# Layer 0's last modulation chunks as sums on VectorE, part of the exponentials' sums on GpSimd, and norms by quarters of the tokens

## Chip, cores and metric

The kernel runs on one core of a Trainium2 chip. The metric is the device time of one execution in microseconds. The engines are called PE (TensorE's matmuls), PEld (its weight loads), DVE (VectorE), ACT (ScalarE), POOL (GpSimd) and SP (SyncE, which issues the transfers here).

## The reference

Two layers work on 512 latent tokens and a prefix of 256 context tokens, 1024 wide, in fp32. Layer 0 is attention (16 query heads, 4 key heads, head size 64), layer 1 a bidirectional Mamba-2 mixer; each is followed by a gated FFN with a short convolution.

```python
for i in range(DEPTH):
    mod_l = split((silu(c) @ ada_w[i] + ada_b[i]), 6)          # shift, scale, gate: mixer, then FFN
    mod_c = split(silu(c_ctx) @ ada_w[i] + ada_b[i], 6)
    h_l = modulate(rms_norm(x, norm_mix_w[i]), mod_l[0], mod_l[1])
    h_c = modulate(rms_norm(ctx, norm_mix_w[i]), mod_c[0], mod_c[1])
    ...                                                        # attention or Mamba-2
    x = x + mod_l[2] * o_l
    x = x + mod_l[5] * conv_ffn(modulate(rms_norm(x, norm_ffn_w[i]), mod_l[3], mod_l[4]))
    ...                                                        # the context likewise, in layer 0
```

In attention, queries and keys are normed per head (`rms_norm` over 64 channels), rotated by their position (latent tokens only), and a softmax runs over 512 latent and 256 context keys for latent queries, over the 256 context keys for context queries.

## The kernel before

Activations lie transposed: 128 channels on the partitions, tokens along the row (512 latent and 256 context columns, T = 768). Products that need fp32 accuracy split each operand in a high and a low part (`split`: ACT rounds to the high part, VectorE or GpSimd subtracts) and make three passes (`mm3`). The instructions of each engine are put in order by a scheduler that follows the program's order as a priority and lets an idle engine take later work; in the first stage the order of PE, ACT and VectorE is that of the program, and `keep_in_program_order` pins single instructions elsewhere.

**Modulation.** Layer 0's chunks 0 and 1 (shift and scale of the mixer) are made by `ada` on PE during the first projections. Chunks 2, 3 and 4 are six further `ada` units in the list `fill`: each loads four tiles of 512 KB from `adaB`, multiplies them with the conditioning vectors `sc32` (eight matmuls of 512 columns into four groups of 32 rows, L128), copies the result (L130), transposes and adds it up with four small matmuls (L134), and adds the bias (`modulation`). Layer 0's chunk 5 and all of layer 1 are made by `ada_dve` during layer 0's FFN: a row of the transposed weight matrix times the conditioning vector, summed along the row on VectorE (L167).

**Norms.** `rstd_rows` makes 1/sqrt(mean of squares). It multiplies each tile of 128 tokens, as the stationary operand, with one or two columns of ones (L236), so that tokens lie on partitions and the following operations are 1 to 12 columns wide (L239 to L244); then it spreads the result (L247) and transposes it back, tile by tile (L253). It is used for the tokens' norms (width 1024 or 2048) and for the heads' norms in `normed`.

**Attention.** Eight pairs of heads (`Pair`). `maxima` makes the scores once in a rough form to find each query's maximum on VectorE (L603). `steps` runs seven steps: scores with the maximum taken off (L673, L675), the exponential on ACT into `pr` (L676, three buffers), and the sum of the exponentials over the key tiles in `acc`, on VectorE: step 1 adds the first two (L681), steps 2 to 5 add to it (L683), step 6 sums the context's (L687). The product with the values (L637) comes a step later; after step 5 PE adds `acc` over the partitions (L643) and the output is divided. Scores and maxima share two PSUM buffers.

Between the steps, `fill.run(us)` takes work from a list: the projections of queries 4 to 7 (L105 to L108 into `ps_q`), the norms of queries and keys (`normed`: squares on ACT, an exchange of rows by four transfers into `qsw` at L532, the rotary products on GpSimd at L533 to L535, the norm, and the product L539), the modulation units, and from pair 6 on the output projection. Its order is `"123a4k5a6a7aaa"`, with `us = 1.75` up to pair 5. Big weight tiles come from one set of ten buffers (`t4`); transfers are issued on SP's queue in order.

Of the kernel before, what the change touches and what calls it, by code (L numbers as in the profile page):

```python
# [7 lines left out]
P = 128  # L8
# [49 lines left out]
CST_IDENT, CST_BLK, CST_SEL, CST_COS, CST_SIN = 0, 128, 130, 132, 132 + L  # L58
NCST = 132 + 2 * L
# [51 lines left out]
def ada(g, src, layer, chunks, m0, nm, big=True):  # L111


    nc = g.nc
    cols = nm * len(chunks) * P
    per = (1024 if big else T) // cols
    st = []
    for k0 in range(0, KT, per):
        n = min(per, KT - k0)
        t = t4(g, "wada") if big else t3(g, "wada")  # L120
        t = t[:, : n * cols].rearrange("p (k a b) -> p k a b", k=n, a=len(chunks))
        nc.sync.dma_start(t.rearrange("p k a b -> p (k a b)"), src[:, k0 * cols : (k0 + n) * cols])
        st += [t[:, k].rearrange("p a b -> p (a b)") for k in range(n)]
    yield 0
    ps = Bank(g, "ps_ada")
    for k in range(KT):
        j = k % 4
        nc.tensor.matmul(ps[32 * j : 32 * j + 32, 0:cols], g.sc32[:, k, :], st[k], start=k < 4, stop=k >= 4)  # L128
    sb = g.t3p.tile([P, 512], F32, tag="t2", bufs=6, name="ada_sb")
    nc.vector.tensor_copy(sb[:, 0:cols], ps[:, 0:cols])  # L130
    yield BREAK
    pt = Bank(g, "ps_adt")
    for i in range(cols // P):
        nc.tensor.matmul(pt[:, 2 * i : 2 * i + 2], sb[:, i * P : (i + 1) * P], g.sel, start=True, stop=True)  # L134
    for i, ch in enumerate(chunks):
        modulation(g, pt[:, 2 * nm * i : 2 * nm * (i + 1)].rearrange("p (m v) -> p m v", v=2), layer, ch, m0, nm)
    yield BREAK
# [15 lines left out]
def ada_dve(g):  # L153


    nc = g.nc
    cb = g.t3p.tile([P, 2 * D], F32, name="cb")
    nc.sync.dma_start(cb, g.I["cflat"].broadcast_to([P, 2 * D]))
    follow(g, nc.scalar.activation(cb, cb, AF.Silu))
    for layer, ch, nv in [(0, 5, 2)] + [(1, ch, 2 if ch < 2 else 1) for ch in range(6)]:  # L160
        md = g.mod[layer][ch]
        for m in range(KT):
            w = g.t3p.tile([P, D], F32, tag="wada", bufs=3, name="wada")
            nc.sync.dma_start(w, g.I["adaT"][(ch + 1 if layer else 0) * KT + m])
            for v in range(nv):
                junk = g.t3p.tile([P, D], F32, tag="junk", bufs=1, name="junk")
                g.tc.keep_in_program_order(nc.vector.scalar_tensor_tensor(  # L167
                    junk, w, 1.0, cb[:, v * D : (v + 1) * D], ALU.mult, ALU.mult, accum_out=md[:, m, v : v + 1]))
                yield
        modulation(g, md[:, :, :nv], layer, ch, 0, KT, nv)  # L170
# [56 lines left out]
def rstd_rows(g, sq, n, cols, width, name, bank):  # L227

    nc = g.nc
    c = cols.shape[-1]
    nt = n // P
    ps = bank(f"ss{name}")
    for t in range(nt):
        nc.tensor.matmul(ps[:, t * c : (t + 1) * c], sq[:, t * P : (t + 1) * P], cols, start=True, stop=True)  # L236
    small = lambda nm: g.p.tile([P, nt * c], F32, tag="rst", bufs=8, name=nm)
    a, y, u = small("rsa"), small("rsy"), small("rsu")
    nc.vector.tensor_scalar(a, ps[:, : nt * c], 1.0 / width, EPS, ALU.mult, ALU.add)  # L239
# [5 lines left out]
    rb = t3(g, f"rb{name}", n=n)  # L245
    wide = lambda v: v.unsqueeze(2).broadcast_to([P, nt * c, P // c])
    nc.vector.scalar_tensor_tensor(rb.rearrange("p (a b) -> p a b", b=P // c), wide(u), 1.5, wide(y), ALU.add, ALU.mult)  # L247
    yield BREAK
    out = []
    for t0 in range(0, nt, 4):  # L250
        pt = bank(f"rsT{name}")
        for t in range(t0, min(nt, t0 + 4)):
            nc.tensor.transpose(pt[:, (t - t0) * P : (t - t0 + 1) * P], rb[:, t * P : (t + 1) * P], g.ident)  # L253
        yield (pt, t0 * P, min(n, (t0 + 4) * P))
# [55 lines left out]
class Norm:  # L310
# [23 lines left out]
    def gen(self, seg, x, lag=2):  # L334

        i, a, b = seg
        g, nc, n = self.g, self.g.nc, b - a
        for _ in range(lag):
            yield
        rows = rstd_rows(g, self.acc[seg, 6], n, g.ones[:, :1], D, self.name, lambda nm: Bank(g, nm))  # L340
        next(rows)
        for _ in range(lag):
            yield
        rs = t3(g, f"rs{self.name}", n=n)
        nc.scalar.copy(rs, next(rows)[0][:, :n])
# [33 lines left out]
def attention(g, fill, X, late):  # L379
# [14 lines left out]
    mods = [ada(g, I["adaA"][m], 0, (0, 1), m, 1, big=False) for m in range(KT)]  # L394
# [26 lines left out]
    nc.sync.dma_start(g.cst, I["cst"][:, :CST_COS])  # L421
# [9 lines left out]
    def warmth(n):  # L431
        for _ in range(n):
            nc.tensor.matmul(warm[:, :P], g.ones, g.ones, start=True, stop=True)
# [8 lines left out]
    norm = rstd_rows(g, acc, L, g.ones[:, :1], D, "a", Bk)  # L442
# [12 lines left out]
    rsl, _, _ = next(norm)  # L455
# [12 lines left out]
    for m in range(KT):  # L468
# [11 lines left out]
        if m == 3:  # L480
            norm = rstd_rows(g, sqc, C, g.ones[:, :1], D, "a", Bk)
            next(norm)
        if m == 4:
            rsc = t3(g, "rsc", n=C)
            pt, _, _ = next(norm)
            nc.scalar.copy(rsc, pt[:, :C])
# [15 lines left out]
    man.__exit__(None, None, None)  # L502
    nc.sync.dma_start(g.cs, I["cst"][:, CST_COS:])

# [20 lines left out]
    def normed(qs, gain, eng):  # L525
# [10 lines left out]
        for r in rstd_rows(g, sq, T, g.blk, HD, "q", Bk):  # L536
            if r is not BREAK:
                pt, c0, c1 = r
                nc.vector.tensor_tensor(qs[:, c0:c1], qs[:, c0:c1], pt[:, : c1 - c0], ALU.mult)  # L539
            yield BREAK  # L540
# [18 lines left out]
    def queries(p, qs, eng):  # L559
# [14 lines left out]
        split(g, qs, *qprep[p])  # L574
        yield 0

    onesr = g.const.tile([P, P], F32R, name="onesr")
    nc.scalar.copy(onesr, g.ones)
# [5 lines left out]
    class Pair:  # L584
# [43 lines left out]
        def steps(self):  # L628
# [10 lines left out]
            def final(po, ps, acc, out):  # L639

                n = out.shape[-1]
                for e in range(2):
                    nc.tensor.matmul(ps[S64[e], :n], g.ones[:, :HD], acc[:, n * e : n * e + n], start=True, stop=True)  # L643
# [22 lines left out]
            for t in range(7):  # L666
                ps, pr = Sb("ps_s"), g.t3p.tile([P, 1024], F32, tag="pr", bufs=3, name="pr")
                for q0, n, k0, off in (((0, L, t * P, 0),) if t < 6 else ((L, C, L, 0), (L, C, L + P, C))):
# [5 lines left out]
                    for e in range(2):  # L674
                        nc.tensor.matmul(outs[e], onesr[S64[e]], self.diag[S64[e], q], start=False, stop=True)  # L675
# [3 lines left out]
                elif t == 1:  # L679
                    acc = g.t3p.tile([P, 1024], F32, tag="acc", bufs=1, name="acc")  # L680
                    nc.vector.tensor_tensor(acc, prev, pr, ALU.add)  # L681
                elif t < 6:
                    nc.vector.tensor_tensor(acc, acc, pr, ALU.add)  # L683
# [10 lines left out]
    for n, j in enumerate((0, 1, 2, 4, 5, 3)):  # L694
# [8 lines left out]
        for gen in early:  # L703
            next(gen, None)
    vals = values()
# [20 lines left out]
    adas = list(fill.q)  # L726
    fill.q = [kgen if o == "k" else adas.pop(0) if o == "a" else qgen[int(o)] for o in "123a4k5a6a7aaa"]
# [151 lines left out]
def ssd(g, x, norm, wf, bg, close):  # L879
# [340 lines left out]
    norm = rstd_rows(g, acc[0], L, g.ones[:, :1], 2 * D, "y", lambda nm: Bank(g, nm))  # L1220
    next(norm)
    m_tile(4, ws, ps, 0, L, range(2 * 4, 16))
    nc.scalar.copy(rs, next(norm)[0])
# [31 lines left out]
def body(nc, tc, I, out, dbg=None):  # L1255
# [20 lines left out]
    g.ident, g.blk, g.sel = (cst[:, a:b] for a, b in  # L1276
                             ((CST_IDENT, CST_IDENT + P), (CST_BLK, CST_BLK + 2), (CST_SEL, CST_SEL + 2)))
    g.ones = g.const.tile([P, P], F32, name="ones")
    nc.vector.memset(g.ones, 1.0)
# [8 lines left out]
    for i in range(6):  # L1288
# [157 lines left out]
```

## Time and profile before

| | us |
|---|---|
| median of 3 runs | 1912.97 |
| lowest, highest | 1905.94, 1915.4 |
| the profiled execution | 1914.7 |
| its span | 1912.9 |

The span is from the first to the last instruction of the profiled execution. Tables of windows give each engine's busy time in a stretch, in us from the start of the span; attention lies in about 5 to 400 us, its head pairs in about 122 to 400 us. Groups are given as line, engine, operation, tile names, shapes and count, then busy time and mean duration in ns, then the idle time before them. Rows of a single line or tile give min/median/max in ns instead. A busy PE counts matmuls as the profile models them.

### The profile page before, as it was taken

The page shows a single profiled execution, that of the slowest core. Times are in us where ns is not written, and L with a number is a line of the kernel's source. Part 1 is how long each engine was busy: PE and PEld are TensorE (multiplying, and loading weights), DVE is VectorE, ACT ScalarE, POOL GpSimd, SP SyncE. Part 2 cuts the span into 40 slices and gives each one's busy share as a digit, 9 for nine tenths or more (in the row PEclk, how much of TensorE's full clock was granted, in tenths as well). Part 3 has the DMA queues.
Part 4 walks back from the last instruction along what each step waited for, and adds up shares of the span by engine and source line. Part 5 has one row for each costly group of instructions (what it writes and reads, how often), then busy time and mean ns, then how long its engine had stood idle before and what let it go on. Part 6 is the DMA issues. An engine that isn't in the chain of part 4 may idle for free.

```text
span 1912.9 us, 27512 instructions
## 1 busy us (share of the span) xinstructions
PE 1876.5 (98%) x10834; PEld 1547.6 (81%) x10834; DVE 1311.2 (69%) x1943; ACT 823.0 (43%) x1426; POOL 309.8 (16%) x274
## 2 busy tenths in 40 slices
PE   9999999999999999999999999999999999999999
PEld 7866555678888888888888888888888878888887
DVE  5578778678877777444488777777888466565555
ACT  3634444255122222222266777776667352323331
POOL 2241111031000000000040344443434210000000
PEclk9989998999999999999999999999999999999999
DMA  9221332114434555221122443334443322323232
GB/s 337 78 89 45 113 112 95 34 45 166 132 122 132 174 188 166 66 67 60 62 89 87 121 118 115 126 113 133 120 138 115 91 77 86 102 88 110 88 100 88
DMA packets 73425, 210.02 MB, mean 110 GB/s; under 512 B 8912, under 2 KB 14416, under 8 KB 73168
## 3 DMA queue, kind: packets, MB, share of 16 engines
q1 hardware_dynamic: 73296, 208.26, 34.3%
q8 instruction: 85, 1.39, 0.3%
q14 instruction: 44, 0.36, 0.1%
HBM read 198.79 MB, written 6.82 MB: 107 GB/s over the span
## 4 chain that ended last, share of the span: by engine, by line
PE 79%; DVE 9%; issue 3%; ACT 2%; POOL 1%; DMA 1%; DVEq 0%; SPq 0%; POOLq 0%; ACTq 0%
PE ps_up L106 10%; PE ps_up L108 10%; PE ps_up L105 10%; PE ps_d L105 6%; PE ps_d L106 6%; PE ps_d L108 6%; PE ps_in L106 4%; PE ps_in L108 4%; PE ps_in L105 4%; PE ps_o L637 2%; PE ps_s L673 2%; PE ps_st L1033 2%; DVE ht L281 1%; PE ps_wo L108 1%; PE ps_wo L105 1%
## 5 line engine op out<-in xcount | busy, mean ns | idle before, releaser
L87 DVE TENSOR_TENSOR wl<-wst,wh 128x1024 fp32r<-128x1024 f32 x205 | 254.5, 1242 | 244.9 <-PE ps_up L106 137.7
L85 ACT CAST wh<-wst 128x1024 fp32r<-128x1024 f32 x211 | 221.2, 1049 | 423.2 <-DMA wst<-in_wup 333.8
L106 PE MATMUL ps_up<-hlf,wh 128*128 128x512 f32 x1008 | 357.0, 354 | 0.0
L105 PE MATMUL ps_up<-hhf,wh 128*128 128x512 f32 x1008 | 356.9, 354 | 0.0
L108 PE MATMUL ps_up<-hhf,wl 128*128 128x512 f32 x1008 | 356.8, 354 | 0.0
L105 PEld LDWEIGHTS ps_up<-hhf,wh 128*128 128x128 f32 x1008 | 190.5, 189 | 26.5
L106 PEld LDWEIGHTS ps_up<-hlf,wh 128*128 128x128 f32 x1008 | 190.6, 189 | 26.4
L108 PEld LDWEIGHTS ps_up<-hhf,wl 128*128 128x128 f32 x1008 | 190.5, 189 | 26.4
L105 PE MATMUL ps_in<-hhs,wh 128*128 128x512 f32 (+1 forms) x560 | 204.4, 365 | 0.0
L106 PE MATMUL ps_in<-hls,wh 128*128 128x512 f32 (+1 forms) x560 | 199.4, 356 | 0.0
L108 PE MATMUL ps_in<-hhs,wl 128*128 128x512 f32 (+1 forms) x560 | 198.7, 355 | 0.0
L105 PE MATMUL ps_d<-hdh,wh 128*128 128x512 f32 (+1 forms) x568 | 193.6, 343 | 1.4 <-DVE X L784 1.2
L108 PE MATMUL ps_d<-hdh,wl 128*128 128x512 f32 (+1 forms) x568 | 193.5, 341 | 0.0
L106 PE MATMUL ps_d<-hdl,wh 128*128 128x512 f32 (+1 forms) x568 | 193.0, 340 | 0.3 <-DVE hdl L87 0.3
L784 DVE SCALAR_TENSOR_TENSOR X<-ps_d,mod,X 128x512 f32<-128x512 f32 (+1 forms) x224 | 124.6, 583 | 36.9 <-PE ps_d L108 36.6
L106 PEld LDWEIGHTS ps_d<-hdl,wh 128*128 128x128 f32 x568 | 106.6, 188 | 14.8 <-DVE hdl L87 0.7
L105 PEld LDWEIGHTS ps_d<-hdh,wh 128*128 128x128 f32 x568 | 106.3, 188 | 14.8 <-DVE X L784 1.4
L105 PEld LDWEIGHTS ps_in<-hhs,wh 128*128 128x128 f32 x560 | 105.9, 189 | 15.1 <-issue 1.2
L108 PEld LDWEIGHTS ps_in<-hhs,wl 128*128 128x128 f32 x560 | 105.8, 189 | 14.8
L108 PEld LDWEIGHTS ps_d<-hdh,wl 128*128 128x128 f32 x568 | 106.7, 188 | 13.1
L106 PEld LDWEIGHTS ps_in<-hls,wh 128*128 128x128 f32 x560 | 106.0, 189 | 13.2
L676 ACT ACTIVATE pr<-ps_s 128x1024 f32<-128x1024 f32 x56 | 57.2, 1021 | 110.6 <-PE ps_s L675 109.6
(340 smaller groups left out, 3547.3 us busy)
## 6 DMA issues: line engine op xcount, KB each, us to landing
wst<-in_wup SPq DMA_DIRECT2D x88, 512.0 KB, 3.6
wada<-in_adaT SPq DMA_DIRECT2D x56, 512.0 KB, 3.9
wst<-in_win SPq DMA_DIRECT2D x48, 512.0 KB, 3.7
wst<-in_wdown SPq DMA_DIRECT2D x44, 512.0 KB, 3.6
E<-ad SPq DMA_DIRECT2D x64, 256.0 KB, 6.8
wada<-in_adaB SPq DMA_DIRECT2D x24, 512.0 KB, 4.6
ec<-ead SPq DMA_DIRECT2D x64, 128.0 KB, 5.0
wst<-in_wout SPq DMA_DIRECT2D x16, 512.0 KB, 3.6
```

What stands on the lines that cost most here:

```text
L85: keep(nc.scalar.copy(hi, src))
L87: keep(eng.tensor_tensor(lo, src, _r(hi), ALU.subtract))
L105: mm(out, wh, ah, start=first, stop=False)
L106: mm(out, wh, al, start=False, stop=False)
L108: mm(out, wl, ah, start=False, stop=last)
L281: nc.vector.scalar_tensor_tensor(t[:, c0:c1], ap, g.moda[layer][ca][:, m, v : v + 1], rs[:, c0:c1], ALU.mult, ALU.mult)
L637: nc.tensor.matmul(po[S64[e], :n], v, pr[:, 512 * e + off : 512 * e + off + n], start=first, stop=last)
L673: nc.tensor.matmul(outs[e], a[S64[e], k], b[S64[e], q], start=i == 0, stop=False)
L676: nc.scalar.activation(pr, ps, AF.Exp)
L784: nc.vector.scalar_tensor_tensor(ap, o[:, c0:c1], gate[:, m, v : v + 1], ap, ALU.mult, ALU.add)
L1033: nc.tensor.matmul(ps[:, d * 256 : (d + 1) * 256], Bt[:, t * P : (t + 1) * P], xw[d][t], start=t == ts[0], stop=t == ts[-1])
```

## The change

- Chunks 2, 3 and 4 of layer 0 are made by `ada_dve`, now a general function: 24 tiles of 512 KB from `adaT`, each multiplied with two vectors and summed on VectorE, 48 instructions. Two vectors `cv` are stored to DRAM from `sc32` and read back onto all partitions. The sums are taken one at a time: one in each of six rounds of the context's projections, one in every fourth step of the values, in steps 0, 1, 2, 3 and 6 of each pair, and in every step of pair 5. They aren't pinned in the program's order.
- The adds of the exponentials in steps 1, 2 and 3 go to GpSimd, and so does the low part of each normed query.
- `fill` holds only queries and keys; `us` is 1.2 up to pair 5.
- The norms change: `rstd_heads` multiplies the squares, as the moving operand, with block columns into four groups of 32 rows (a quarter of the tokens each, 192 columns), works on 192 columns, and spreads the result with four matmuls against a selecting matrix `pick`. `rstd_quarters` does so for 512 tokens. `rstd_all` (the norms of context and FFN inputs) multiplies with a full matrix of ones and works on the whole width, with no transposes and no copy.
- Matrices of ones are one column, read with a step of zero.

```diff
-def ada_dve(g):
+def ada_dve(g, chunks, c, tile, pin):
+    nc = g.nc
+    for layer, ch, nv in chunks:
+        md = g.mod[layer][ch]
+        for m in range(KT):
+            w = tile("wada")
+            nc.sync.dma_start(w, g.I["adaT"][(ch + 4 if layer else ch - 2) * KT + m])
+            for v in range(nv):
+                junk = tile("junk") if v < nv - 1 else w
+                i = nc.vector.scalar_tensor_tensor(junk, w, 1.0, c[v], ALU.mult, ALU.mult, accum_out=md[:, m, v : v + 1])
+                if pin:
+                    g.tc.keep_in_program_order(i)
+                yield
+        modulation(g, md[:, :, :nv], layer, ch, 0, KT, nv)
...
-def rstd_rows(g, sq, n, cols, width, name, bank):
+def rsqrt_mean(g, ps, width, name):
...
+    n = ps.shape[-1]
+    w = t3(g, f"rs{name}", n=3 * n)
+    a, y, u = (w[:, i * n : (i + 1) * n] for i in range(3))
+    nc.vector.tensor_scalar(a, ps, 1.0 / width, EPS, ALU.mult, ALU.add)
...
     nc.vector.tensor_tensor(u, y, a, ALU.mult)
     nc.vector.scalar_tensor_tensor(u, y, -0.5, u, ALU.mult, ALU.mult)
+    nc.vector.scalar_tensor_tensor(a, u, 1.5, y, ALU.add, ALU.mult)
+    return a
+
+def rstd_all(g, sq, width, name):
+    n = sq.shape[-1]
+    ps = Bank(g, f"ss{name}")[:, :n]
+    g.nc.tensor.matmul(ps, g.ones(P), sq, start=True, stop=True)
+    return rsqrt_mean(g, ps, width, name)
+
+def sums_by_group(g, sq, cols, name):
+    n = sq.shape[-1] // 4
+    ps = Bank(g, f"ss{name}")[:, :n]
+    for j in range(4):
+        g.nc.tensor.matmul(ps[32 * j : 32 * j + 32], cols, sq[:, j * n : (j + 1) * n], start=True, stop=True)
+    return ps
...
+def rstd_heads(g, sq, name):
+    n = T // 4
+    r = rsqrt_mean(g, sums_by_group(g, sq, g.blk, name), HD, name)
+    yield BREAK
+    pt = [Bank(g, f"rsT{name}") for _ in range(2)]
+    for i in range(2):
+        for e in range(2):
+            rows = slice(64 * e, 64 * e + 64)
+            g.nc.tensor.matmul(pt[e][:, i * n : (i + 1) * n], g.pick[rows, i * P : (i + 1) * P], r[rows],
+                               start=True, stop=True)
+    yield [(pt[e], 2 * e * n, 2 * e * n + 2 * n) for e in range(2)]
...
+    cd = g.dp.tile([2, D], F32, name="cd")
+    cv = [t4(g, "cv") for _ in range(2)]
+    for v in range(2):
+        nc.sync.dma_start(cd[v].rearrange("(k p) -> p k", p=P), g.sc32[:, :, v])
+        nc.sync.dma_start(cv[v], cd[v : v + 1].broadcast_to([P, D]))
+    adas = ada_dve(g, [(0, ch, 2) for ch in (2, 3, 4)], cv, lambda name: t4(g, name), False)
...
-        split(g, qs, *qprep[p])
+        split(g, qs, *qprep[p], lo_engine="pool")
...
-                    nc.vector.tensor_tensor(acc, prev, pr, ALU.add)
+                    nc.gpsimd.tensor_tensor(acc, prev, pr, ALU.add)
                 elif t < 6:
-                    nc.vector.tensor_tensor(acc, acc, pr, ALU.add)
+                    (nc.gpsimd if t < 4 else nc.vector).tensor_tensor(acc, acc, pr, ALU.add)
...
+        if n in (0, 1, 2, 3, 4, 5):
+            next(adas, None)
...
-    fill.q = [kgen if o == "k" else adas.pop(0) if o == "a" else qgen[int(o)] for o in "123a4k5a6a7aaa"]
+    for o in "1234k567":
+        fill.add(kgen if o == "k" else qgen[int(o)])
...
+        if i % 4 == 1:
+            next(adas, None)
...
-        us = 1.75 if p < 6 else 2.9
+        us = 1.2 if p < 6 else 2.9
         for t, todo in enumerate(pairs[p].steps()):
             next(m, None)
+            if t in (0, 1, 2, 3, 6) or p == 5:
+                next(adas, None)
```

More of the change, by code (lines that the diff above doesn't have):

```diff
@@ L159, in ada_dve @@
     follow(g, nc.scalar.activation(cb, cb, AF.Silu))
[L160 to L170, printed above, removed]
+    tile = lambda name: g.t3p.tile([P, D], F32, tag=name, bufs=3 if name == "wada" else 1, name=name)
+    yield from ada_dve(g, [(0, 5, 2)] + [(1, ch, 2 if ch < 2 else 1) for ch in range(6)],
+                       [cb[:, :D], cb[:, D:]], tile, True)
 BREAK = object()
@@ L393, in attention @@
     man.__enter__()
[L394 removed]
+    mods = [ada(g, m) for m in range(KT)]
     W6 = 6 * P
@@ L480, in attention @@
         if m == 3:
[L481 to L486, printed above, removed]
+            rsc = rstd_all(g, sqc, D, "a")
         for j in range(6):
@@ L535, in normed @@
         eng.tensor_tensor(qs[:, :L], qs[:, :L], sw, ALU.add)
[L536 to L540, printed above, removed]
+        rows = rstd_heads(g, sq, "q")
+        yield next(rows)
+        for pt, c0, c1 in next(rows):
+            nc.vector.tensor_tensor(qs[:, c0:c1], qs[:, c0:c1], pt[:, : c1 - c0], ALU.mult)
+        yield BREAK
     k2 = {}
@@ L1219, in ssd @@
     ln_exp(g)
-    norm = rstd_rows(g, acc[0], L, g.ones[:, :1], 2 * D, "y", lambda nm: Bank(g, nm))
+    norm = rstd_quarters(g, acc[0], 2 * D, "y")
     next(norm)
     m_tile(4, ws, ps, 0, L, range(2 * 4, 16))
-    nc.scalar.copy(rs, next(norm)[0])
+    nc.scalar.copy(rs, next(norm))
     for i in range(4):
```

112 lines of the change are left out of this document (49 added, 63 removed).

## The prediction

> **What bounds the kernel now.** I read the first part of the profile's page, then a table of windows, then the waits, the groups by line and form, and the timeline in attention.
>
> ```profile
> span 1912.9 us, 27512 instructions
> ## 1 busy us (share of the span) xinstructions
> PE 1876.5 (98%) x10834; PEld 1547.6 (81%) x10834; DVE 1311.2 (69%) x1943; ACT 823.0 (43%) x1426; POOL 309.8 (16%) x274
> ```
>
> TensorE is the bound on average. Nearly everything in this change lies in attention, so the windows come next. Their columns are the length, the busy time of PE, PEld, DVE, ACT and POOL with their counts, the granted clock, the DMA share and GB/s.
>
> ```profile
> 75.00:122.00 47.00, 43.12 (x338) 40.12 (x340) 30.64 (x45) 21.27 (x37) 14.75 (x10) 0.96 0.36 111
> 122.00:306.00 184.00, 181.70 (x1148) 103.78 (x1146) 144.74 (x202) 79.83 (x109) 36.14 (x21) 0.95 0.30 100
> 306.00:400.00 94.00, 91.50 (x535) 59.26 (x532) 71.79 (x112) 35.03 (x50) 0.00 (x0) 1.00 0.15 48
> 300.00:325.00 25.00, 23.61 (x128) 12.78 (x125) 23.82 (x42) 14.14 (x24) 0.00 (x0) 0.98 0.23 74
> 1420.00:1475.00 55.00, 53.29 (x282) 44.27 (x281) 49.00 (x56) 41.56 (x88) 27.92 (x22) 1.00 0.37 117
> 292.00:301.00 9.00, 9.00 (x34) 5.29 (x31) 5.58 (x12) 3.29 (x5) 1.19 (x1) 0.50 0.19 75
> ```
>
> The first row holds the context's projections, the first key and query norms and the values; the second the head pairs 0 to 5; the third pairs 6 and 7 with the output projection. In 75 to 306 (231 us) PE is busy 224.8 us, VectorE 175.4 us (76%) and GpSimd 50.9 us (22%). So PE sets the pace there, VectorE has 56 us of idle time, and GpSimd is nearly free. The waits of the pairs agree:
>
> ```profile
> ACT pr L676 <- PE ps_s L675: 67.4, 32, 4.8
> POOL qs L533 <- DVE rsu L243: 38.0, 1, 38.0
> POOL qs L533 <- DMA qsw<-qs: 36.3, 3, 21.1
> ```
>
> ScalarE's exponentials wait for the scores on PE. GpSimd's long waits cost nothing now, because nothing is queued behind them.
>
> **What leaves PE.** The groups of 75 to 306 by line and form (count, busy time, mean ns, idle), and one matmul elsewhere with 192 columns in fp32 (min/median/max ns, first and last start):
>
> ```profile
> L236 PE MATMUL ssq<-cst,qsq 128*128 128x2 f32 x114 | 15.2, 260 | 0.3 <-ACT qsq L528 0.3
> ...
> L128 PE MATMUL ps_ada<-wada,sc 128*32 128x512 f32 x96 | 14.0, 671 | 0.0
> ...
> L253 PE MATMUL rsTq<-cst,rbq 128*128 128x128 f32 x58 | 9.9, 286 | 2.9 <-DVE rbq L247 2.9
> ...
> L134 PE MATMUL ps_adt<-cst,ada_sb 128*128 128x2 f32 x48 | 7.7, 285 | 0.0
> ```
> ```profile
> L1144 PE MATMUL ps_end<-acsT,cst x4: 326/326/429, 1035.0 to 1035.6; 128*128 128x192 f32 x4
> ```
>
> The six modulation units leave with all of L128 and L134: 21.7 us. The ten head norms now take 15.2 + 9.9 = 25.1 us, 2.5 each. After it a norm is four matmuls of 192 columns into four groups of 32 rows, and four more that broadcast the result from two halves of the rows. The L1144 row is two matmuls of 192 columns in four records, over about 0.93 us, so 0.46 us each. I take the four sums as one such time, since the L128 rows show four column groups side by side (eight matmuls of 512 columns in 14.0/6 = 2.3 us, when 2.67 times 0.46 us for each would make 9.8 us), and the broadcasts as two: 1.4 us. That frees 1.1 us for each of ten, 11 us; if nothing ran side by side, 3.7 us each, and 12 us would be lost. The window 292 to 301 has PE at half clock with 9.00 of 9 us busy: 4.5 us that come from the light matmuls of the last modulation units, and go with them. So PE gets 21.7 + 11 + 4.5 = 37 us in this stretch (14 at least, with the 12 lost). If PE alone set the pace, that would be the gain.
>
> On this clock the Trainium skill (TensorE: Matmul & The Clock Gate, Part 1) states that idleness halves it and sustained work restores it. A PE that is busy all through, as in that row, would keep its clock by this reading, and the 4.5 us would not be on offer; the trace shows the half clock beside full busy time.
>
> **What VectorE gets and gives.** The groups of 75 to 306 that the change touches, then one operation with 192 columns, then the sums that layer 0's FFN already does in the new manner:
>
> ```profile
> L603 DVE TENSOR_REDUCE ma<-ps_m 128x2 f32<-128x1024 f32 x28 | 34.2, 1221 | 18.4 <-PE ps_m L601 18.3
> L683 DVE TENSOR_TENSOR acc<-acc,pr 128x1024 f32<-128x1024 f32 x24 | 30.2, 1258 | 2.9 <-ACT pr L676 2.9
> ...
> L247 DVE SCALAR_TENSOR_TENSOR rbq<-rsu,rsy 128x768 f32<-128x768 f32 x10 | 11.7, 1173 | 0.4
> ...
> L681 DVE TENSOR_TENSOR acc<-pr 128x1024 f32<-128x1024 f32 x6 | 7.3, 1212 | 0.0
> L243 DVE TENSOR_TENSOR rsu<-rsy,rsa 128x12 f32<-128x12 f32 x10 | 7.0, 702 | 2.9 <-ACT rsy L241 2.9
> ...
> L130 DVE COPY ada_sb<-ps_ada 128x512 f32<-128x512 f32 x6 | 4.1, 687 | 2.4 <-PE ps_ada L128 2.4
> ...
> L87 DVE TENSOR_TENSOR ql<-raw,qh 128x768 fp32r<-128x768 f32 x4 | 3.8, 955 | 2.0 <-ACT qh L85 2.0
> ...
> L87 DVE TENSOR_TENSOR ql<-qs,qh 128x768 fp32r<-128x768 f32 x3 | 2.9, 954 | 0.9 <-ACT qh L85 0.9
> ...
> L239 DVE TENSOR_SCALAR rsa<-ssq 128x12 f32<-128x12 f32 x10 | 1.7, 165 | 11.2 <-PE ssq L236 11.0
> ```
> ```profile
> L1157 DVE TENSOR_TENSOR dw<-ps_end,acsT x2: 347/352/356, 1042.9 to 1043.2; 128x192 f32<-128x192 f32 x2
> ```
> ```profile
> L167 DVE SCALAR_TENSOR_TENSOR junk<-wada,cb 128x1024 f32<-128x1024 f32 x80 | 97.2, 1216 | 1.2 <-ACT cb L159 0.8
> L167 DVE DVE_READ_ACCUMULATOR junk<-wada,cb 128x1 f32 x80 | 6.5, 81 | 0.0
> ```
>
> Added: 48 sums (three chunks, eight blocks, two vectors) at 1.216 + 0.081 us: 62.3 us. By the code's own order six stand in the context loop, twelve in the values, five in each of pairs 0 to 4 and the last five in pair 5, so all lie in 75 to 306. Removed in this stretch: the exponentials' adds of steps 1 to 3, six at 1.212 and twelve at 1.258 us, 22.4 us; the queries' low parts, 3.8 + 2.9 = 6.7 us; the copies of L130, 4.1 us. A norm was three short operations of 0.165 us and one wide one of about 0.96 us where nothing is in its way (the ql rows, equally wide): 1.45 us. It becomes four of 0.35 us, 1.4 us: no difference. Net: 62.3 - 33.2 = +29 us, so 175.4 becomes 204.5 us of 231.
>
> **What GpSimd gets, and what that does to VectorE.** Its own rates are in one line's view of the weight splits:
>
> ```profile
> L87 POOL TENSOR_TENSOR wsl<-wst,wsh x7: 1817/1830/1841, 14.6 to 54.5; 128x768 fp32r<-128x768 f32 x7
> L87 POOL TENSOR_TENSOR wl<-wst,wh x6: 2365/2382/2831, 75.9 to 206.2; 128x1024 fp32r<-128x1024 f32 x6
> ```
>
> Eighteen adds at 2.38 and seven low parts at 1.83 us are 55.7 us more, so 50.9 becomes 107 us of 231. That alone would fit. But the two engines stand in each other's way. From the timeline:
>
> ```profile
> 121.93 2.37 POOL L87 TENSOR_TENSOR wl<-wst,wh 128x1024 fp32r<-128x1024 f32 x1
> ...
> 122.23 2.09 DVE L243 TENSOR_TENSOR rsu<-rsy,rsa 128x12 f32<-128x12 f32 x1 [0.24 <-ACT rsy L241]
> ```
>
> A VectorE operation on 12 columns takes 2.09 us and ends when GpSimd's split ends (124.32 against 124.30): while GpSimd works, VectorE's operations with two operands from SBUF stand still. The price so far can be read from the groups: L243 took 7.0 us where ten of 0.165 us are 1.7 (5.3 lost), L247 11.7 against 9.6 (2.1), L683 30.2 against 24 of 1.212 (1.1). That is 8.5 us for 50.9 us of GpSimd, a sixth, and the smaller groups add to it. VectorE will be fuller, and the new GpSimd operations longer, so I take a third: 18 us for the 55.7 us. The bounds are a sixth (9 us) and the share in the pair of rows above, 2.09 of 2.37 (49 us). VectorE then needs 204.5 + 18 = 223 us (214 to 254).
>
> Can it be filled so far? The fullest stretch of the trace in which PE goes on is 300 to 325: VectorE 23.82 of 25, 0.95. At that rate 223 us need 234 us; at the 0.89 of 1420 to 1475, 250 us. The stretch takes 231 us now: +3. So the time that PE gets is taken up by VectorE's waits for its port, and the stretch stays as long as it is.
>
> **The rest.** In 306 to 400 six adds move to GpSimd, 7.4 us off a VectorE that is busy 71.79 of 94; PE has 2.5 us of idle time left to win there, and I take 2. The other norms (the first ones, the FFN's, the SSD's) lose their transposes and a copy and get operations on 128 or 256 columns for such of 1 to 8; the 0.35 us of the L1157 row against 0.165 makes four or five of them 0.8 us dearer, and the wide one, the transposes and the copy about as much cheaper: 0, within 2. The conditioning vector now goes to DRAM and comes back spread over the rows, twice, on SP's queue ahead of the first key's swap. The nearest transfers are the heads' outputs, out and back (KB, median us to landing):
>
> ```profile
> odram<-o SPq DMA_DIRECT2D x6, 384.0 KB, 2.4
> od<-odram SPq DMA_DIRECT2D x6, 384.0 KB, 5.8
> ```
>
> That is 8.2 us at most for each, 0 if it ends ahead of the first key norm; the code makes the vector before its first projection, so I take 0. The 24 big weight loads stay 24. Each edit of constants (ones and the block masks as broadcast columns) changes no count of instructions.
>
> Sum: +3 - 2 = +1 on the 1914.7 us of the profiled execution. This execution lies 1.7 us above the 1912.97 us median of the runs shown, so 1914; as PE's 37 us also shorten the places where VectorE now waits for PE, I shade it by 2 us: **1912 us**, no change.
>
> **Rivals.** *Part of PE's gain survives.* If the sums fall into VectorE's 56 us of waits and GpSimd's adds run beside the maxima, which read PSUM and are in nobody's way, only the sixth is lost: 204.5 + 9 = 214 us. Filled to 0.97 that is 220 us, -11; with the -2 of the last pairs 1900 us. If the half clock and the stalls at the pair borders go too, 1888 us. For it: 37 us of PE work are really gone, and the sums are not pinned, so they can be put where VectorE is idle. Against it: the largest group of maxima, L603 above, is 34.2 us, and GpSimd has 107 us to place.
>
> *VectorE and GpSimd take turns, and this is the new bound (slower).* Place: steps 1 to 3 of each pair, where an add of 2.38 us on GpSimd stands beside a maximum and a sum on VectorE. If each add blocks VectorE for 60% of its length, the price is 33 us instead of 18, VectorE needs 238 us, and at 0.95 the stretch takes 250 us, +19: 1930 us. It decides from a blocked share of about 45% on (230 us, 242 at 0.95, +11). Behind the blocked VectorE stand the maxima, which hold one of two score buffers, so PE waits too. The Trainium skill (SBUF — State Buffer, Who interferes with whom) states this as a rule: the port that VectorE shares with GpSimd is an exclusive lock for a whole instruction. The two timeline rows agree with it, and by it alone this rival would be the forecast.
>
> *A late transfer holds GpSimd's queue.* The adds are now queued behind the rotary products, which wait for the swapped queries (up to 21.1 us above); behind a late add wait VectorE's add of step 4, the sum on PE and one of three exponential buffers. SP's queue can cause it:
>
> ```profile
> 268.98 9.10 SPq L122 DMA_DIRECT2D wada<-in_adaB  x4
> ```
>
> Four loads held SP 9.1 us because their buffers were not free. Two or three such stalls of 4 to 5 us: 1925 us.
>
> **How the numbers follow.** Forecast 0.37, the gain that survives 0.33, turns on the port 0.2, a held queue 0.1. About 0.5% (9.6 us) is what a measurement of this kernel can tell from no change. Faster than 1903.4 us is the first rival nearly whole and a little of the forecast: 0.34. Slower than 1922.5 us is the third and most of the fourth case: 0.29. The rest, 0.37, is no change. The forecast's own range is 1903 to 1922. The whole range reaches to 1888 and 1934, which leaves out about a tenth on each side.
>
> **What would show it.** Right: L128 with 512 columns gone, PE's busy time in attention some 30 us lower but the attention no shorter; VectorE over 90% busy from 75 to 306; short operations of VectorE stretched to 1 or 2 us beside GpSimd's adds; PE's waits in the pairs naming VectorE's maxima. Wrong towards faster: VectorE under 90% with pairs of 28 us or less. Wrong towards slower: pairs over 32 us, or GpSimd's adds waiting for `qsw`.

## The result, and the profile after

The changed kernel takes 2008.11 us (median; 2003.43 to 2010.71), the kernel before 1911.53 us beside it: 1.0515 times as long (95% interval 1.0498 to 1.0532). The forecast of no change was wrong, and its range ended 74 us too low. The page of the profile after, its first lines:

```profile
span 2001.6 us, 27280 instructions
## 1 busy us (share of the span) xinstructions
PE 1877.8 (94%) x10642; PEld 1541.4 (77%) x10642; DVE 1385.6 (69%) x1997; ACT 828.0 (41%) x1417; POOL 369.8 (18%) x306
```

The span grew by 88.7 us, PE's busy time by 1.3. So the time is in waits, and the place of a wait has to be found first. I cut both traces at the same events: the first `ps_c` matmul (the context's projection), the last `ps_v` matmul (the values), the start of each pair's `o<-ps_o,y` on DVE, and first and last `ps_in` (the SSD stage). Up to the context's projection there are 63.2 us before and 92.5 after (+29.3), from there to pair 5's `o` 248.1 and 288.9 (+40.8), in pair 6 42.5 and 53.0 (+10.5), in the SSD stage 423.3 and 431.6 (+8.3); every other stage agrees within 0.5 us. Windows of the kernel before (length, busy PE, PEld, DVE, ACT, POOL with counts, granted clock, DMA share, GB/s):

```profile
22.00:49.00 27.00, 25.05 (x156) 17.80 (x155) 14.26 (x35) 9.13 (x19) 7.32 (x4) 0.94 0.84 322
63.20:311.30 248.10, 240.54 (x1583) 155.59 (x1581) 183.49 (x264) 113.31 (x168) 53.85 (x34) 0.96 0.29 95
```

and of the changed one:

```profile
22.00:49.00 27.00, 3.68 (x27) 2.10 (x25) 0.71 (x1) 2.78 (x6) 1.80 (x1) 0.64 0.76 256
92.50:381.40 288.90, 232.97 (x1409) 143.98 (x1407) 242.13 (x317) 116.15 (x167) 113.37 (x59) 0.90 0.24 78
```

In the first stage the engines stand nearly still for these 27 us (PE is busy for 3.68 of them). The timeline says why:

```profile
30.94 2.69 SPq L542 DMA_DIRECT2D cd<-sc  x2
41.88 1.57 SPq L543 DMA_DIRECT2D cv<-cd  x2
43.55 0.38 SPq L160 DMA_DIRECT2D wada<-in_adaT  x1
44.02 1.37 SPq L120 DMA_DIRECT2D wada<-in_adaA  x3
49.37 1.22 DVE L163 SCALAR_TENSOR_TENSOR junk<-wada,cv 128x1024 f32<-128x1024 f32 x1 [26.66 <-DMA wada<-in_adaT]
50.52 0.75 DVE L332 SCALAR_TENSOR_TENSOR hla<-ht,mod,hha 128x512 fp32r<-128x512 f32 x1
51.32 0.80 PE L107 MATMUL ps_l<-hla,wsh 128*128 128x512 f32 x1 [25.64 <-DVE hla L332]
```

The first sum, which the program asks for during the context's projection, stands on DVE's queue ahead of the second latent low part (`hla`). DVE ran them in that order: it waited 26.66 us for the sum's vector and weights, and PE 25.64 us for the low part, which stood behind the sum. On SP's queue the broadcast of the vector waits for its store, and layer 0's last weight loads of the first chunks (`in_adaA`) wait behind both.

In the long stage VectorE is busy for 58.6 us more and PE waits for it (us in all, times, longest):

```profile
PEld ps_m L642 <- DVE ma L644: 21.5, 9, 7.5
PE rsTq L293 <- DVE rsq L247: 18.2, 6, 6.3
PE ps_m L642 <- DVE ma L644: 17.3, 8, 7.1
PEld ps_s L716 <- DVE diag L665: 12.0, 5, 3.8
```

Pair 0's timeline shows what those waits are made of:

```profile
165.63 2.56 DVE L246 SCALAR_TENSOR_TENSOR rsq<-rsq 128x192 f32<-128x192 f32 x1
167.92 2.50 POOL L88 TENSOR_TENSOR wl<-wst,wh 128x1024 fp32r<-128x1024 f32 x1
168.12 2.52 DVE L245 TENSOR_TENSOR rsq<-rsq 128x192 f32<-128x192 f32 x1
170.38 2.45 POOL L724 TENSOR_TENSOR acc<-acc,pr 128x1024 f32<-128x1024 f32 x1
170.56 2.49 DVE L247 SCALAR_TENSOR_TENSOR rsq<-rsq 128x192 f32<-128x192 f32 x1
...
175.64 1.21 DVE L644 TENSOR_REDUCE ma<-ps_m 128x2 f32<-128x1024 f32 x1
176.78 0.34 DVE L241 TENSOR_SCALAR rsq<-ssq 128x192 f32<-128x192 f32 x1
176.91 0.79 PE L642 MATMUL ps_m<-kh,qh 64*128 64x256 f32 x4 [7.06 <-DVE ma L644]
```

With GpSimd's operations back to back, VectorE gets one operation in between two of them: three steps of a head norm, 0.36 us each when nothing is in the way, take 2.5 us each, a maximum comes behind them, and PE stands for 7 us. The maximum and the step L241, which read PSUM, keep their 1.21 and 0.34 us.

### The profile page after: what moved, and what is told of

Read it like the earlier page. It is cut to its first block, busy times and chain, and to the rows that moved or that the text cites. A ratio compares the mean times of both kernels' runs of the same rounds, so it can differ in the third digit from the quotient of the medians.

```text
span 2001.6 us, 27280 instructions
## 1 busy us (share of the span) xinstructions
PE 1877.8 (94%) x10642; PEld 1541.4 (77%) x10642; DVE 1385.6 (69%) x1997; ACT 828.0 (41%) x1417; POOL 369.8 (18%) x306
## 4 chain that ended last, share of the span: by engine, by line
PE 64%; DVE 13%; issue 4%; ACT 2%; DMA 2%; POOL 2%; SPq 0%; DVEq 0%; POOLq 0%; ACTq 0%
PE ps_up L107 10%; PE ps_up L106 10%; PE ps_up L109 10%; PE ps_d L106 6%; PE ps_d L107 6%; PE ps_d L109 6%; DVE xf L1010 3%; PE ps_in L109 3%; PE ps_in L107 3%; PE ps_in L106 3%; DVE Bf L1010 1%; DVE wl L88 1%; PE ps_o L678 1%; PE ps_wo L106 1%; PE ps_wo L109 1%
## 5 line engine op out<-in xcount | busy, mean ns | idle before, releaser
L107 PE MATMUL ps_up<-hlf,wh 128*128 128x512 f32 x1008 | 357.0, 354 | 0.0
L107 PEld LDWEIGHTS ps_up<-hlf,wh 128*128 128x128 f32 x1008 | 190.6, 189 | 26.3
L107 PE MATMUL ps_in<-hls,wh 128*128 128x512 f32 (+1 forms) x560 | 199.9, 357 | 0.0
L107 PE MATMUL ps_d<-hdl,wh 128*128 128x512 f32 (+1 forms) x568 | 193.0, 340 | 0.3 <-DVE hdl L88 0.3
L107 PEld LDWEIGHTS ps_d<-hdl,wh 128*128 128x128 f32 x568 | 106.7, 188 | 14.8 <-DVE hdl L88 0.7
L106 PEld LDWEIGHTS ps_in<-hhs,wh 128*128 128x128 f32 x560 | 106.2, 190 | 15.1 <-issue 1.0
L107 PEld LDWEIGHTS ps_in<-hls,wh 128*128 128x128 f32 x560 | 106.3, 190 | 13.5
```

Of the source, the lines that this page charges most:

```text
L106: mm(out, wh, ah, start=first, stop=False)
L107: mm(out, wh, al, start=False, stop=False)
```

## The experiments

The table has the median, its ratio to the kernel before with the interval, and, from the profiled execution, the stages in us: up to the context's projection, that projection with the values, pair 0, pairs 1 to 5, pair 6, SSD. These come from one execution each: e11_ffn_norm has the attention code of the kernel before, and its pairs 0 to 5 are 7.7 us shorter, so less than 8 us in pairs 0 to 5 is not read as a difference. About half of that is the granted clock: all engines have the same instructions in the same order there, and one run of PE's in pair 5 takes 8.8 us in the kernel before, at 0.52, and 4.9 in e11_ffn_norm, at 1.00:

```profile
292.60:301.40 8.80, 8.80 (x35) 5.41 (x32) 5.83 (x10) 2.91 (x4) 0.59 (x1) 0.52 0.13 48
```
```profile
289.60:294.50 4.90, 4.90 (x35) 3.03 (x31) 4.34 (x10) 3.29 (x5) 2.63 (x2) 1.00 0.65 250
```

The SSD stage is steadier: 423.1 to 424.0 us wherever the norms ahead of it are as before. Each ratio is to the kernel before as measured beside that run (medians of 1908.4 to 1911.5 us), so differences between rows in us carry up to 3 us of that.

| kernel | us | ratio | start | ctx, values | p0 | p1-5 | p6 | SSD |
|---|---|---|---|---|---|---|---|---|
| before | 1908.4 to 1911.5 | 1 | 63.2 | 55.0 | 33.3 | 159.8 | 42.5 | 423.3 |
| after | 2008.11 | 1.0515 | 92.5 | 60.9 | 48.7 | 179.3 | 53.0 | 431.6 |
| e3_sum_late | 1983.85 | 1.0386 [1.0369, 1.0403] | 72.2 | 61.4 | 48.6 | 177.8 | 53.4 | 432.7 |
| e4_both_late | 1977.73 | 1.0364 [1.0336, 1.0392] | 63.6 | 61.1 | 48.5 | 177.2 | 53.6 | 436.0 |
| e8_fill_175 | 1960.78 | 1.0265 [1.0248, 1.0282] | 65.9 | 61.1 | 48.7 | 174.4 | 40.0 | 435.4 |
| e7_no_gpsimd | 1965.92 | 1.0291 [1.0271, 1.0311] | 65.5 | 61.7 | 40.5 | 168.2 | 53.5 | 437.3 |
| e12_no_gpsimd_fill | 1953.28 | 1.0241 [1.0224, 1.0258] | 65.4 | 61.4 | 46.7 | 165.6 | 41.3 | 431.9 |
| e10_even_sums | 1968.53 | 1.0309 [1.0292, 1.0325] | 67.1 | 56.9 | 43.9 | 175.9 | 54.2 | 434.6 |
| e1_norms | 1926.28 | 1.0082 [1.0054, 1.011] | 65.7 | 54.0 | 33.9 | 154.6 | 41.3 | 434.0 |
| e6_y_rows | 1928.25 | 1.0084 [1.0063, 1.0105] | 67.0 | 53.1 | 34.2 | 156.0 | 41.3 | 438.9 |
| e11_ffn_norm | 1925.88 | 1.0091 [1.0073, 1.0109] | 62.8 | 56.5 | 30.8 | 154.6 | 42.5 | 439.8 |
| e5_heads | 1908.91 | 0.9993 [0.998, 1.0005] | 61.4 | 52.9 | 34.2 | 158.0 | 41.3 | 423.9 |
| e2_pool | 1924.83 | 1.0075 [1.0057, 1.0093] | 62.9 | 55.3 | 33.0 | 163.3 | 49.3 | 423.1 |
| e9_sums_alone | 1938.7 | 1.0155 [1.014, 1.017] | 61.8 | 61.5 | 43.5 | 170.3 | 42.5 | 423.2 |
| e14_even_alone | 1934.97 | 1.0118 [1.0097, 1.0139] | 61.5 | 55.6 | 35.5 | 171.7 | 48.6 | 424.0 |
| e13_half_sums | 1915.65 | 1.0022 [1.0009, 1.0035] | 61.6 | 56.3 | 37.6 | 153.5 | 42.5 | 424.0 |
| e15_best_of_it | 1926.93 | 1.0071 [1.005, 1.0093] | 61.9 | 55.6 | 38.5 | 167.5 | 39.8 | 423.5 |

**The first stage.** A dependency that only orders instructions of one engine puts the sums, the first one with them, behind the last `hla` of the first stage (both runs), and the vector's stores behind the last `in_adaA` load on SP (second run).

```diff
+                if not pin:
+                    behind(g, i, g.first_end)      # e3, e4: sums after the first stage's last hla
...
+        behind(g, i, g.last_ada)                   # e4: cd stores after the last adaA load
```

> The changed kernel with its first sum put behind the last VectorE instruction of the first stage; stores and transfers as they are. Theory that VectorE stood still for the first sum's data: the 26.7 us wait goes, and with it about 29 us: 1976 to 1983 us. Rival, that SyncE's queue did it (two stores of the vector and their broadcasts stand ahead of nine weight loads of layer 0's first chunks): only part comes back, 1985 to 2000 us, and the context projection still starts 10 us or more later than in the kernel before.

> As the run before it, and the stores of the vector put behind the last of those nine weight loads on SyncE's queue. Theory of the sum alone: no different from the run before it, within 4 us. Rival of SyncE's queue: 8 to 20 us below it. By both the first projection ends within 3 us of the kernel before (context projection from 63 us on), and what is left to 1912, some 60 us, lies in the pairs and 8 us in the SSD stage.

Both causes are real: the sum costs 20.3 us of the start (92.5 to 72.2), the stores 8.6 (to 63.6). In time that is 24.3 us (2008.1 to 1983.9) and 6.1 us (to 1977.7); each result lies between the ranges of its theory and its rival. The last two ratios' intervals overlap; in the five runs with both edits and the change's norms the start is at 63.6 to 67.1 us, 5 to 9 us ahead of the 72.2. How long the two stores of 4 KB were on their way, in the DMA issues of the kernel after (KB, median us to landing):

```profile
cd<-sc SPq DMA_DIRECT2D x2, 4.0 KB, 11.3
```

SP could not issue the broadcast before that. In the ten other kernels with these stores each took 10.2 to 12.4 us, in e4_both_late with no other transfer moving in the last 5 us of it. The heads' outputs, 96 times as large, land in 2.4 us by the rows of the prediction. The store writes runs of 4 bytes; the Trainium skill (DMA: Bandwidth & Descriptors, Specifications) puts the smallest transfer for full rate at 512 bytes, which goes the same way, though no run here varied the run's length alone.

**GpSimd's part.** Alone on the kernel before; then taken off the changed kernel with a repaired start.

```diff
-                    nc.vector.tensor_tensor(acc, prev, pr, ALU.add)
+                    nc.gpsimd.tensor_tensor(acc, prev, pr, ALU.add)    # e2; steps 2, 3 and the low parts of queries too
```

> The kernel before with the first three adds of each pair and the queries' low parts on GpSimd, nothing else. Theory that VectorE and GpSimd hold each other up: short VectorE operations beside the 2.4 us adds stretch, pairs 0 to 5 get longer by 1 to 3 us each: 1918 to 1930 us. Rival, that VectorE is only relieved (29 us less work) and TensorE sets the pace: 1905 to 1915 us.

> The changed kernel with first sum and stores late, and all adds and low parts back on VectorE: sums and norms alone. Theory that the two engines hold each other up: pairs 0 to 3 (48.5, 37.1, 37.6, 33.1 us with GpSimd's work) get shorter by 2 to 6 us each, pair 6 falls from 53.6 to 44 us: 1950 to 1965 us. Rival, that VectorE's plain amount of work decides (29 us more of it in a stage in which it is busy for 47.1 of 48.5 us): pairs 0 to 3 longer by 3 to 5 us each, 1985 to 2000 us.

Alone it costs 0.75%, and the amount of VectorE's work explains neither result. Windows of the same stage in e2_pool, e4_both_late and e7_no_gpsimd:

```profile
62.90:314.50 251.60, 241.94 (x1583) 155.78 (x1583) 169.44 (x234) 114.06 (x169) 107.69 (x59) 0.96 0.28 90
```
```profile
63.60:350.40 286.80, 232.75 (x1409) 144.52 (x1407) 242.96 (x320) 116.25 (x167) 115.84 (x59) 0.89 0.24 79
```
```profile
65.50:335.80 270.30, 225.00 (x1409) 138.49 (x1407) 244.47 (x345) 116.25 (x167) 57.88 (x34) 0.93 0.26 83
```

29.1 us of adds and low parts (22.4 and 6.7 in the prediction) left VectorE in the first, but only 14.1 us of busy time (183.5 to 169.4): 15.0 us came back as blocking, 28% of the 53.8 us that GpSimd got. In the changed kernel the same 29.1 us of work are worth 1.5 us of busy time (244.5 against 243.0): 27.6 us of blocking, 48% of 58.0 us. The share is higher where VectorE is fuller; these are two kernels, which differ in more than VectorE's load. e7's stage is 16.5 us shorter with more work on VectorE, so the rival there falls. In the changed kernel pair 6 did not move (53.5), so its loss has another cause. In e2_pool, at the old budget of the next experiment, pair 6 is 6.8 us longer with a granted clock of 0.90 (before 1.00); why was not taken further.

**The query work between the steps.** `fill.run` got 1.2 us a step after, 1.75 before.

```diff
-        us = 1.2 if p < 6 else 2.9
+        us = 1.75 if p < 6 else 2.9
```

> The changed kernel with first sum and stores late, and 1.75 us of query work between steps as before in place of 1.2. Theory that the next query's chain is late at the pair's start (TensorE waits for the norm's broadcast, 10.2 us in all, and for the maxima): 1 to 2 us less in each of pairs 1 to 6, 1965 to 1973 us. Rival, that VectorE bounds pairs 0, 2 and 3 whatever TensorE does: 1974 to 1982 us.

> The changed kernel with first sum and stores late, all adds and low parts on VectorE and 1.75 us of query work between steps. If the two gains add (17 us by GpSimd's relief in pairs 0 to 3, 13 us in pair 6 by the query work): 1946 to 1954 us, pair 6 at 40 to 42 us. Rival, that pairs 1 and 2 lose with the longer fill what pair 6 gains (they went from 37 to 42 us beside GpSimd's adds): 1957 to 1966 us.

Pair 6 falls from 53.6 to 40.0 us (41.3 in e12) and pair 5 from 38.8 to 30.2, pairs 1 and 2 lose 9 us of it, the whole gains 17.0 us: more than either range. That the smaller budget leaves the last queries' work to the borders of the late pairs is the reading; shown is that this number costs pair 6 its 11 us. With GpSimd's work gone as well 7.5 us more come back (the two ratios' intervals overlap), less than the 11.8 without the longer fill.

**The norms.** All of them on the kernel before; all but y's; those ahead of FFN and mixer alone; the head norms alone (with the change's constants).

```diff
-        rows = rstd_rows(g, self.acc[seg, 6], n, g.ones[:, :1], D, self.name, lambda nm: Bank(g, nm))
-        next(rows)
+        rs = rstd_all(g, self.acc[seg, 6], D, self.name)        # e11: in Norm.gen, nothing else
```

> The kernel before with the norms of the change alone (modulation on TensorE, adds and low parts on VectorE as before). Theory that the norms are a small gain of TensorE time in attention (ten head norms, 2.5 to 1.4 us each): 1900 to 1911 us, FFN and SSD as before. Rival, that the 8 us lost in the SSD stage belong to the norm of y by quarters, and some of attention's loss to the head norms' chain (four 192-column steps on VectorE ahead of a broadcast that TensorE waits for): 1918 to 1930 us, with first to last ps_in near 431 us in place of 423.

> The norms of the change without the norm of y, which is done as before. If the norm of y by quarters lengthens the SSD stage: ps_in back at 423 us, 1907 to 1914 us. Rival, that the short norms ahead of the SSD stage (one all-ones matmul and a t3 buffer of their own in place of two) put the scheduler's order of that stage out: ps_in stays at 431 to 436 us, 1917 to 1930 us.

> The kernel before with the norms ahead of FFN and mixer alone as one all-ones matmul and wide steps. If these norms put the SSD stage out: first to last ps_in 431 to 439 us in place of 423, attention as before: 1917 to 1930 us. If it takes the other norms too: 423 us, 1906 to 1913 us.

> The kernel before with the ten head norms of keys and queries by quarters, every other norm as it was. If the second run's loss (first to last ps_in 434 us in place of 423) sits in the other norms and its gain (393.6 to 389.3 us at pair 7's end, with 2.5 us lost in the first stage) in the head norms: SSD back at 423 us, pair 7 ends at 386 to 389 us, the whole 1897 to 1906 us, faster than the kernel before. Rival, that any shift in attention moves the SSD stage: 1912 to 1922 us.

The head norms do what they were said to do on PE, in e5_heads (61.4 to 306.6 us):

```profile
L286 PE MATMUL rsTq<-rsq,cst 64*128 64x192 f32 x80 | 10.0, 348 | 5.0 <-DVE rsq L240 3.0 <-DVE raw L605 2.0
L259 PE MATMUL ssq<-qsq,cst 128*32 128x192 f32 x80 | 5.3, 338 | 0.5 <-ACT qsq L594 0.5
```

1.5 us a norm in place of 2.5, and yet the time is the same (0.9993, 0.998 to 1.0005), between the two expected ranges. The loss of norms belongs to the FFN's and mixer's: alone they lengthen an SSD stage whose code is not changed at all, from 423.3 to 439.8 us, and with y's norm as before it is still 438.9. The expectation that y's norm did it was wrong. The SSD windows of the kernel before and of e11_ffn_norm, and PE's longest wait in each:

```profile
1009.90:1433.20 423.30, 420.53 (x2479) 364.19 (x2479) 322.98 (x377) 291.76 (x617) 152.67 (x133) 1.00 0.41 119
```
```profile
1004.50:1444.30 439.80, 425.75 (x2479) 367.35 (x2479) 333.82 (x378) 292.20 (x617) 139.64 (x134) 0.99 0.39 115
```
```profile
PE ps_xt L1007 <- DVE xf L1110: 1.9, 6, 0.5
PE ps_xt L1029 <- DVE ec L1122: 10.3, 6, 2.5
```

The same matmuls, but PE idle for 14 us in place of 3, 10.3 of them for `ec` on VectorE, for which it does not wait before. The instructions stand in another order there: against the kernel before, 148 of VectorE's 377 places in this stage and 178 of PE's 2480 hold another instruction (by operation, tiles and shape). The traces show just two orders: the old one in the seven kernels with the old norms ahead of FFN and mixer (423.1 to 424.0 us), one other in the ten with the new ones (431.6 to 439.8). Which buffer or estimate turned the order over was not tried.

**The sums themselves.** On the kernel before, with first sum and stores late and 1.75 us of fill; then half of them; then their place.

```diff
-            for v in range(nv):
+            for v in range(nv if pin else 1):      # e13: no sums for the context, whose values are the latents'
...
-        if n in (0, 1, 2, 3, 4, 5):                # e10, e14: no sums beside context and values,
-            next(adas, None)                       # one at every step of pairs 0 to 6
```

> The kernel before with the modulation as sums on VectorE alone: first sum and stores late, 1.75 us of query work between steps, every norm, add and low part as before. Theory that the sums make VectorE's queue late for short operations that TensorE waits for: context projection 34 to 37 us in place of 27.4, pairs 0 to 3 longer by 8 to 16 us together although TensorE has 21.7 us less to do, SSD at 423 us: 1925 to 1942 us. Rival, that the loss needs the new norms or GpSimd's work beside them: 1890 to 1910 us.

> The kernel with the sums alone (1938.7 us), and only every other sum done: the context's modulation takes the latents' value, so 24 sums, some 31 us of VectorE, are left out at the same pace of asking. If each sum costs its share (in front of something that TensorE waits for): pairs 0 to 4, 191 us with all sums and 156 us before, fall to 168 to 178 us: 1915 to 1926 us. Rival, that the loss comes from TensorE losing the modulation matmuls that filled its waits, however many sums: 1932 to 1942 us.

> The changed kernel with first sum and stores late, and its sums asked for evenly, one at each of seven steps of pairs 0 to 6, none beside the context projection and the values. Theory that the sums in front of the head norms cost the 8.6 us of the context projection, and their crowding the 15 us of pair 0: context projection back at 27 to 28 us, pair 0 at 38 to 42 us in place of 48.5, later pairs 1 to 3 us longer: 1958 to 1970 us. Rival, that the scheduler takes sums when it likes, or that they cost the same wherever they lie: 1974 to 1982 us.

> The kernel with the sums alone, asked for evenly over pairs 0 to 6 and none earlier. If place matters as it did in the whole change (9 us): context projection 27 to 28 us, values 25 to 28, pairs 0 to 4 185 to 195 us: 1926 to 1934 us. Rival, that without GpSimd's adds the place makes no difference: 1936 to 1942 us.

The same stage in e9_sums_alone and in e13_half_sums:

```profile
61.80:337.00 275.20, 246.66 (x1439) 155.74 (x1438) 241.89 (x351) 115.73 (x170) 62.74 (x34) 0.91 0.28 88
```
```profile
61.60:309.10 247.50, 224.87 (x1439) 145.90 (x1437) 216.03 (x307) 114.45 (x170) 57.71 (x34) 0.97 0.31 97
```

With all sums 1938.7 us, with half 1915.65. By the ratios the kernel with 24 sums, which leaves out the context's, 31 us of work, is 4 us over the kernel before (0.22%, interval 0.09 to 0.35), and the second 24 add 25 us (1.55% less 0.22%). The first 24 are not free for that. In this stage PE is busy for 15.7 us less than before (240.54 to 224.87) and idle for 15.1 us more (7.6 to 22.6): waits took up what the modulation's matmuls had left. Two readings fit both times: some 25 us for each 24 sums, less one relief of 21 us, near the 21.7 us of these matmuls; or a limit of VectorE, which is busy for 0.88 and 0.87 of these stages (it reaches 0.92 in e12_no_gpsimd_fill). No run tells them apart. What sums in the queue do is seen in e4_both_late's context projection (35.9 us in place of 27.4):

```profile
82.75 1.22 DVE L163 SCALAR_TENSOR_TENSOR junk<-wada,cv 128x1024 f32<-128x1024 f32 x1
...
84.83 0.35 DVE L253 TENSOR_TENSOR rsq<-rsq 128x192 f32<-128x192 f32 x1
85.10 1.22 DVE L163 SCALAR_TENSOR_TENSOR wada<-wada,cv 128x1024 f32<-128x1024 f32 x1
...
86.24 0.69 DVE L584 TENSOR_TENSOR raw<-raw,cs 128x512 f32<-128x512 f32 x1
86.85 0.68 DVE L585 TENSOR_TENSOR qsw<-qsw,cs 128x512 f32<-128x512 f32 x1
87.45 0.35 DVE L254 SCALAR_TENSOR_TENSOR rsq<-rsq 128x192 f32<-128x192 f32 x1
87.72 0.68 DVE L586 TENSOR_TENSOR raw<-raw,qsw 128x512 f32<-128x512 f32 x1
87.81 2.79 POOL L88 TENSOR_TENSOR wl<-wst,wh 128x1024 fp32r<-128x1024 f32 x1 [8.51 <-DVE rsq L254]
88.32 2.50 DVE L255 SCALAR_TENSOR_TENSOR rsq<-rsq 128x192 f32<-128x192 f32 x1
90.96 1.65 PE L301 MATMUL rsTq<-rsq,cst 64*128 64x192 f32 x8 [6.28 <-DVE rsq L255]
```

Two sums stand among the steps of a head norm; its last step then falls beside GpSimd's split, is held by it, and PE stands 6.28 us before the broadcast. In e10_even_sums, with no sums here, the projection takes 27.1 us. Without sums in these stages they take 56.9 us in place of 61.1 (e10), 55.6 in place of 61.5 (e14), and the whole 9.2 us less in the changed kernel, but only 3.7 us (7 by the ratios; between the two expected ranges) in the kernel with sums alone, where pair 6 takes up 6 us: place is worth something, the amount more.

**What is left of the change at its best.** Even sums, head norms by quarters, everything else as before.

> Sums evenly over pairs 0 to 6, head norms by quarters, all other norms as before, adds and low parts on VectorE, 1.75 us of query work, first sum and stores late: everything of the change that did not lose by itself, with the sums. If the losses found are all there are: SSD 423 us, start 63 us, attention 10 to 25 us over the kernel before: 1920 to 1934 us. If the sums can be hidden after all: under 1909 us.

1926.93 us, within the range of the first theory: the losses found are nearly all there are, and in no version tried were the sums hidden. No version beat the kernel before; e5_heads equals it.

## Why the prediction was wrong, step by step

- **"All lie in 75 to 306" and "the code makes the vector before its first projection, so I take 0".** This step failed first, for 30 of the 96 us. The document itself says that the scheduler lets an idle engine take later work; the sums are not pinned, and I used that only as a chance for gain. A queue in order turned it round: the unpinned sum stood ahead of work that was due, and the stores ahead of loads that were. My bound for a store and its way back, 8.2 us, came from large transfers and had 2.4 us for the store; the store alone took 11.3.
- **VectorE's work.** +29 us was right as work. The blocked share was taken as a third, 18 us, with 9 to 49 as bounds: alone it is 28% (e2_pool), in the changed kernel 48%, 27.6 us. So in the changed kernel the share is one at which the rival, turns on the port, decides (from 45%), though its 1930 us was still 78 us short; the step that failed was to read the share from a trace in which VectorE was 74% busy. By the Trainium skill (SBUF — State Buffer, Who interferes with whom) a VectorE instruction with two SBUF inputs contends with a GpSimd instruction that reads SBUF, and one with at most one SBUF input, outside the two-port modes, does not; the 2.50 us of L255 and the unmoved 0.34 of L241 agree with it.
- **"At that rate 223 us need 234 us."** The step that failed worst. The 0.95 came from 300 to 325, where PE had 10.6 us of output projection (`ps_d`) between the pairs' work and waited only 1.1 us for maxima. In this stage PE waits for short results of VectorE (maxima, head norms, diagonals), and VectorE reached 0.84 (242.13 of 288.90), without GpSimd's work 0.90 (0.92 with the longer fill), with sums alone 0.88. At 0.95 the measured 242.13 us would have been 255, 7 us over the stage before; it was 41. Which short result costs how much was not separated.
- **PE's 37 us.** The matmuls went (x1583 to x1409), and the head norms alone gave 10 of their 11 us. But PE's busy time in the stage fell by only 7.6 us, while the granted clock fell from 0.96 to 0.90: behind its waits PE is slower (L107 took 0.40 us ahead of the first stage's wait, 0.80 right behind it). The 4.5 us for the half clock were no gain to be had: e11_ffn_norm runs the same matmuls in the same order at 1.00 (the two windows under the experiments), so these matmuls alone do not bring the half clock.
- **Pairs 6 and 7, -2.** The fill's 1.75 to 1.2 us was in the diff and in no term; it cost pair 6 its 10.5 us.
- **The other norms, 0 within 2.** What the instructions themselves cost was not measured apart; the miss is in the stage behind them: SSD +8.3 us, in the other order.
- **The signs.** Of those named, the missing L128, the stretched short operations and PE's waits on maxima came; VectorE over 90% and PE 30 us lower did not. Of the signs of a slower kernel, pairs over 32 us came: five of pairs 0 to 5 take 34.0 to 48.7 us (three took 32.3 to 37.3 before). GpSimd's waits for `qsw`, the third rival, were 16 us in all with the longest 5.0, less than before, and no run shows a loss by them.

From the runs the way back is: first sum 24 us, stores 6, fill 17, GpSimd 7.5, then all norms but the heads' and the sums' place 26 together, and 16 us that the sums keep.

## What to carry to other kernels

Work that is not pinned can be put ahead of work that is due: before counting where an added instruction will lie, ask what its engine's queue holds behind it and when its data come. An engine with idle time on average is not free when the bound engine waits for its short results: here 24 sums took up in waits what PE had gained, and 24 more cost 25 us for 31 us of work, although VectorE was busy for no more than 0.92 of this stage in any run. And cost every number in the diff, a budget between steps too.

## What was not expected of the hardware

Two stores of 4 KB in runs of 4 bytes took 11.3 us to land (10.2 to 12.4 over all runs), where 384 KB took 2.4. The share of GpSimd's time that blocks VectorE is no constant: 28% with VectorE 67% busy (169.44 of 251.60), 48% with 85% (242.96 of 286.80). PE's granted clock fell with its own waits, to 0.64 in the first stage's standstill and 0.90 over the long stage; but it also stood at 0.52 beside a PE busy for 8.80 of 8.80 us in one execution, and at 1.00 for the same instructions in another.
